# W_o and the third part of x and C, each by seven products, in a float32 encoder block on one core

## The chip, the cores and the metric

The kernel runs on one core of a Trainium2 chip. Its time is the device time of one execution in microseconds (us). Before the change the median of three runs is 1026.59 us (1026.17 to 1027.6). The core has five engines with queues of their own, each served in order: TensorE (PE in the profile, with its weight loads as PEld), VectorE (DVE), ScalarE (ACT), GpSimd (POOL) and SyncE (SP). SP only issues DMAs here. POOL issues DMAs too, among them those that add what they carry to what lies at the destination.

## What is computed

One layer of an encoder on x of 512 tokens by 1024 features, all float32. The parts that the change touches, from the reference:

```python
h = rmsnorm(x, g_mix); proj = h @ w_in
xc, gb, gc, q, k, v, g_sw, gate_a, gate_r = split(proj)
u = gc * xc
conv = sum(u_pad[:, tap:tap + s] * w_conv[tap] for tap in range(3))
y_a = (gb * conv) @ w_a_out
ret = retention forward + backward over 4 heads of q, k, v
y_r = (groupnorm(ret) * silu(g_sw)) @ w_r_out
m = sigmoid(gate_a) * y_a + sigmoid(gate_r) * y_r
x = x + m @ w_o
h2 = rmsnorm(x, g_ffn)
x = x + (silu(h2 @ w_ff_gate) * (h2 @ w_ff_up)) @ w_ff_down
return rmsnorm(x, g_final)
```

## The kernel before

**Products.** Every float32 operand is kept as a high and a low part, hi + lo, and a product takes three matmuls: hi·hi, hi·lo, lo·hi. `split` makes the two parts: ScalarE casts to hi (L200), VectorE subtracts to get lo (L201). Matmuls write PSUM banks of 128 x 512, of which there are eight.

**Seven products.** Much of the work is done on 2 x 2 quarters by Strassen's scheme in Winograd's form: seven products of quarters in place of eight, at the price of sums of quarters of both operands (named s1 to s4 for the activations, t1 to t4 for the weights) and of the results. `strassen` (L434) does it token-major with 512 columns (the value and gate quads, W_a, `down`): 24 matmuls of 512 columns per product. `fm_quad` (L383) does it feature-major through `prod` (L372): 24 matmuls of 256 columns per product. W_o (L1037 to L1058) and the third and fourth part of the convolution (`do_mix`, L801) are plain: W_o has 192 matmuls of 512 columns, and x, C and B of one part 48 each.

**Weights.** `plan` lists all units of weights in the order of use. A "q" entry is one quarter or sum of quarters, a "c" entry a plain block of two units. SP loads them into ten `raw` tiles of 128 x 1024 (512 KB; L283 for quarters, L240 for blocks), some `LEAD` = 4 entries ahead. For a sum like t1 = b11 + b12 VectorE adds two raw tiles (L298). Then `split` fills one of five `whi` and `wlo` buffers. A raw tile comes free when its remainder is made, a whi/wlo pair when its last matmul is done.

**Sums made in DRAM.** For the quads named in `SUMMED` (the first two of the feed-forward, `("f", 0)` and `("f", 1)`) the sums t1 to t4 are made ahead by DMAs on POOL's queue: eight steps a quad, a copy (L271) and then an adding copy (L269) for each of four sums. Each step is queued behind a store of a value or gate quad (`sum_step`, called at L745 and L754): three per quad, six quads.

**Order.** Value and gate quads (to about 324 us), the convolution's first two parts (`mix_quads`: x and C of part 0, of part 1, B of both), loads of head 0 and its scores, part 2 (`do_mix(2)`), then per head the product with v, group norm (POOL takes the power -1/2, L890) and the product with W_r, W_a by `strassen`, merge, W_o, feed-forward, final norm. The order of instructions on each engine is set by a list scheduler when the program is built, from the order in which the code makes them and the readiness it models; `tc.issue_after` adds an edge on one engine.

**W_o before.** `turn(0)` and `turn(1)` transpose the merged m on TensorE (L981) and split it out of PSUM. Four banks collect each half of W_o. For each block of 128 tokens `ev_o` adds the residual (L1003), stores the row block, takes squares on ScalarE, a power on POOL, and scales (L1015); `tr_o` transposes the normed block (L1030) and makes its parts (L1033 to L1035) for the feed-forward, whose first products are `first_tokens`. One block of W_o lies in a `big` tile in place of whi/wlo buffers. There are fourteen `big` tiles, and nine `t` tiles of 128 x 512.

## Time and profile before

| | |
|---|---|
| Median of 3 runs | 1026.59 us |
| The profiled execution | 1027.93 us, its span 1026.1 us |
| TensorE busy | 1018.1 us, 99% of the span, 5610 matmuls |
| VectorE busy | 886.3 us, 86% |
| ScalarE busy | 535.5 us, 52% |
| GpSimd busy | 125.0 us, 12% |
| Granted TensorE clock | 0.999 |

The profile is one execution. A page gives busy time by engine, the chain that ended last, and groups of instructions; the trace behind it can be asked for waits, for stretches of time and for single instructions. A name such as "L201 DVE TENSOR_TENSOR wlo<-raw,whi" is line 201 on VectorE, writing `wlo` from `raw` and `whi`. A busy matmul includes its pipeline, so successive matmuls overlap in the rows, and their rate is read from the chain.

### The profile page before, as it was taken

To read this page: it belongs to the slowest core of one execution; us is meant where nothing else is said; L and a number is where in the kernel's file an instruction comes from. 1 tells how busy PE (TensorE), PEld (TensorE's weight loads), DVE (VectorE), ACT (ScalarE), POOL (GpSimd) and SP (SyncE) were. 2 spreads that over 40 slices of the span, in tenths; PEclk is the share of its full clock that TensorE was granted. 3 is DMA by queue.
4 is the path that set the end of the run, shared out by engine and by line. 5 is a ranking of instruction groups with operands and counts; after the bars stand their busy time and mean duration, and the time that the engine had idled before them with its cause. 6 is when DMAs were issued, how large, how long until landed. Compare 5 with 4: busy or idle time off the path is not lost.

```text
span 1026.1 us, 14780 instructions
## 1 busy us (share of the span) xinstructions
PE 1018.1 (99%) x5610; PEld 887.9 (87%) x5610; DVE 886.3 (86%) x1151; ACT 535.5 (52%) x728; POOL 125.0 (12%) x205
## 2 busy tenths in 40 slices
PE   9999999999999999999999999999999999999997
PEld 7888888888888998888888888889998999899986
DVE  7878998969798988797999998569998999889996
ACT  7547655553656455342542334356654565556554
POOL 0030231222212003202011000000002000110011
PEclk9999999999999999999999999999999999999999
DMA  9525597794767657828177525633318522663513
GB/s 346 195 83 183 172 299 211 213 312 153 255 203 238 254 200 256 323 81 314 52 277 285 208 94 176 236 102 121 122 44 220 177 87 83 193 156 103 164 29 96
DMA packets 51304, 187.66 MB, mean 183 GB/s; under 512 B 6880, under 2 KB 7008, under 8 KB 47264
## 3 DMA queue, kind: packets, MB, share of 16 engines
q1 hardware_dynamic: 36448, 133.19, 37.5%
q0 software_dynamic: 14496, 53.23, 17.5%
q8 instruction: 44, 0.72, 0.3%
q10 hardware_dynamic: 288, 0.29, 0.1%
q14 instruction: 28, 0.23, 0.1%
HBM read 148.14 MB, written 46.92 MB: 190 GB/s over the span
## 4 chain that ended last, share of the span: by engine, by line
PE 97%; DVE 1%; DMA 1%; issue 0%; POOL 0%; ACT 0%; POOLq 0%; DVEq 0%; ACTq 0%
PE bank L424 34%; PE bank L380 28%; PE bank L339 11%; PE bank L341 11%; PE bank L340 11%; DMA raw<-wquad 1%; PE bank L470 0%; PE bank L1030 0%; PE bank L981 0%; PE bank L655 0%; DVE wlo L201 0%; DVE raw L298 0%; DVE big L1229 0%; DVE t L445 0%; POOL fin L1219 0%
## 5 line engine op out<-in xcount | busy, mean ns | idle before, releaser
L200 ACT CAST whi<-raw 128x1024 fp32r<-128x1024 f32 (+2 forms) x291 | 294.5, 1028 | 278.7 <-PE bank L424 60.0
L201 DVE TENSOR_TENSOR wlo<-raw,whi 128x1024 fp32r<-128x1024 f32 (+2 forms) x292 | 343.9, 1193 | 81.6 <-ACT whi L200 81.1
L380 PE MATMUL bank<-xform,whi 128*128 128x256 f32 x1424 | 257.6, 284 | 0.2 <-ACT whi L200 0.2
L380 PEld LDWEIGHTS bank<-xform,whi 128*128 128x128 f32 x1424 | 222.4, 192 | 1.2 <-ACT t L431 0.5
L380 PE MATMUL bank<-xform,wlo 128*128 128x256 f32 x712 | 201.5, 283 | 0.0
L424 PE MATMUL bank<-whi,big 128*128 128x512 f32 x596 | 187.6, 390 | 0.0
L298 DVE TENSOR_TENSOR raw<-raw 128x1024 f32<-128x1024 f32 (+1 forms) x128 | 152.1, 1206 | 3.8 <-DMA raw<-wquad 2.8
L380 PEld LDWEIGHTS bank<-xform,wlo 128*128 128x128 f32 x712 | 136.8, 192 | 0.0
L424 PEld LDWEIGHTS bank<-whi,big 128*128 128x128 f32 x596 | 112.0, 188 | 23.8 <-ACT t L431 0.4
L424 PE MATMUL bank<-whi,xform 128*128 128x512 f32 x384 | 121.3, 390 | 0.0
L424 PE MATMUL bank<-wlo,big 128*128 128x512 f32 x298 | 116.2, 390 | 0.0
L431 ACT COPY t<-bank 128x512 f32<-128x512 f32 x105 | 61.0, 585 | 56.3 <-PE bank L380 29.7
L339 PE MATMUL bank<-big,whi 128*128 128x512 f32 x220 | 85.8, 390 | 0.0
L341 PE MATMUL bank<-big,wlo 128*128 128x512 f32 x220 | 85.7, 390 | 0.0
L340 PE MATMUL bank<-big,whi 128*128 128x512 f32 x220 | 85.7, 390 | 0.0
L424 PEld LDWEIGHTS bank<-whi,xform 128*128 128x128 f32 x384 | 72.1, 188 | 15.1 <-DVE xform L201 0.2
L424 PE MATMUL bank<-wlo,xform 128*128 128x512 f32 x192 | 74.8, 390 | 0.0
L339 PE MATMUL bank<-whi,big 128*128 128x512 f32 x176 | 69.0, 392 | 0.0
L340 PE MATMUL bank<-wlo,big 128*128 128x512 f32 x176 | 68.6, 390 | 0.0
L341 PE MATMUL bank<-whi,big 128*128 128x512 f32 x176 | 68.2, 390 | 0.0
L424 PEld LDWEIGHTS bank<-wlo,big 128*128 128x128 f32 x298 | 56.0, 188 | 11.4
L340 PEld LDWEIGHTS bank<-big,whi 128*128 128x128 f32 x220 | 41.3, 188 | 8.6
(205 smaller groups left out, 1394.8 us busy)
## 6 DMA issues: line engine op xcount, KB each, us to landing
raw<-wquad SPq DMA_DIRECT2D x132, 512.0 KB, 4.6
raw<-wpack SPq DMA_DIRECT2D x50, 512.0 KB, 5.3
z<-t POOLq DMA_DIRECT2D x24, 256.0 KB, 4.7
zform<-z POOLq DMA_DIRECT2D x6, 1024.0 KB, 6.0
v<-t POOLq DMA_DIRECT2D x16, 256.0 KB, 5.3
sg<-t POOLq DMA_DIRECT2D x16, 256.0 KB, 5.0
qh<-t POOLq DMA_DIRECT2D x16, 256.0 KB, 3.0
ql<-t POOLq DMA_DIRECT2D x16, 256.0 KB, 3.6
```

The costliest lines, as they stand in the source:

```text
L200: first = (round or nc.scalar.copy)(hi, src)
L201: nc.vector.tensor_tensor(out=lo, in0=src, in1=hi.bitcast(F32), op=ALU.subtract)
L298: nc.vector.tensor_tensor(out=t, in0=t, in1=raws[quad, more, u][:, 0:n], op=ALU.add)
L339: nc.tensor.matmul(ps, lh, rh, start=first, stop=False)
L340: nc.tensor.matmul(ps, lh, rl, start=False, stop=False)
L341: nc.tensor.matmul(ps, ll, rh, start=False, stop=last)
L380: nc.tensor.matmul(o, l[:, c], r[:, k], start=start and s == 0 and k == 0 and i == 0, stop=stop and k == 3 and i == 2, skip_group_check=True)
L424: nc.tensor.matmul(pss[tt], l, r[:, c], start=start and k == 0 and i == 0, stop=stop and k == n - 1 and i == 2, skip_group_check=True)
L431: nc.scalar.copy(t, ps)
```

## The change

Both plain products become seven. For x and C of part 2, `xc_quad(2)` runs as a third `fm_quad` behind B of the first parts; `do_mix(2)` is left with B of part 2. For W_o, `behind` hooks into `strassen` of W_a: behind its s3 product m's a11 is transposed, behind its a22 product m's a22, then W_o's first product runs, then m's a21 is transposed and s1 and s2 are formed, ahead of W_a's last product. The other five products of W_o follow, with the transposes of a12 inside the second. `turn` now makes one quarter, and `form`, which was the feed-forward's, makes a sum of quarters and its parts. Each product's result goes to the residual by `join` at once, and `complete` does what `ev_o` did when a row block's half is whole.

Both weights join `SUMMED`. The sums of x and C go first among those behind the value and gate quads, and a step now stands behind every second store (four per quad). W_o's sixteen steps stand behind the sixteen powers of the heads. Head 0 is loaded behind `xc_quad(2)`, and weight blocks after that are queued behind its second load (`behind` in `prefetch_block`). All W_o units use the whi/wlo buffers.

```diff
-    for c0, c1 in ((C_XC, C_GC), (C_XC + 256, C_GC + 256), (C_GB, C_GB + 256)):
+    for c0, c1 in ((C_XC, C_GC), (C_XC + 256, C_GC + 256), (C_GB, C_GB + 256), XC[1:]):
         for name in FORMS:
             out.append(("q", ("x", c0, c1), name, 0, 4))
     for s in (2, 3):
-        for c in (C_XC, C_GC, C_GB):
+        for c in (C_GB,) if s == 2 else (C_XC, C_GC, C_GB):
             a("w_in", c + s * 256)
     for h in range(HEADS):
         for c in (0, 512):
             b("w_r_out", h * VD, 4, c, 512)
-    for name in FORMS:
+    for kind, name in [("a", x) for x in FORMS[:6]] + [("o", "b11"), ("a", "b22")] + [
+            ("o", x) for x in ("t1", "t2", "b21", "b22", "t3", "t4")]:
         for u in (0, 2):
-            out.append(("q", ("a",), name, u, 2))
-    for r in (0, 512):
-        for c in (0, 512):
-            b("w_o", r, 4, c, 512)
+            out.append(("q", (kind,), name, u, 2))
...
-SUMMED = (("f", 0), ("f", 1))
+SUMMED = (XC, ("f", 0), ("f", 1), ("o",))
...
+            with tc.issue_after(behind[-1].ins) if behind else nullcontext():
+                nc.sync.dma_start(st[c], wpack[i][:, c * QH:(c + 1) * QH])
...
+    def sums_of(quads):
+        return [(quad, f, g, u, add) for group in (
+            (("t1", "b11", 0), ("t3", "b22", 0)), (("t1", "b12", 1), ("t3", "b12", 1)),
+            (("t2", "t1", 0),), (("t2", "b22", 1),), (("t4", "t2", 0),), (("t4", "b21", 1),))
+            for quad in quads for f, g, add in group for u in parts(quad)]
+
+    steps = {"quads": sums_of(SUMMED[:1]) + sums_of(SUMMED[1:3]), "heads": sums_of(SUMMED[3:])}
+
+    def sum_step(behind, among="quads"):
+
+        if steps[among]:
...
+        if behind:
+            behind(5)
         prod_tm(n, forms["a22"], a, False, True)
         for tt in range(2):
             ev21(tt, a[tt])
...
-                if tt and not o:
+                if tt:
...
+    def xc_quad(s, c):
+
+        u, got = u_tile(), {}
+
+        def ev21(ps):
+            nc.vector.tensor_tensor(out=u[:, :, 257:513], in0=halves(ps), in1=halves(got["c2"]), op=ALU.mult)
+
+        def ev12(t):
+            nc.vector.tensor_tensor(out=u[:, :, 1:257], in0=halves(got["x1"]), in1=halves(t), op=ALU.mult)
+        fm_quad(xf, lambda t: got.update(x1=t), ev21, lambda t: got.update(c2=t), ev12)
+        for m in range(2):
+            conv(m, 2 * s + m, u[:, m], c[:, m])
...
+        part2.append(bigtile()[:, 0:2, :])
+        xc_quad(2, part2[0])
+        head = load_head(0)
+
+        behind.append(last[1])
+        return head
+
+    def do_mix(s):
+        if s == 2:
+            c = part2[0]
...
+            power = nc.gpsimd.tensor_tensor(out=mv[:, 3:4], in0=mv[:, 2:3], in1=mhalf[:, 0:1], op=ALU.pow)
+            sum_step(power, "heads")
...
+        name = f"a{th + 1}{half + 1}"
+        if not m32:
+            t = [bigtile(), bigtile()]
+            for j in range(4):
+                m32[f"a{j // 2 + 1}{j % 2 + 1}"] = t[j // 2][:, j % 2 * 2:j % 2 * 2 + 2, :].rearrange(
+                    "p a (b c) -> p (a b) c", c=256)
+        if name != "a21":
+            M[name] = form_tile()
+        for tt in range(2):
             ps = bank()
             for k in range(4):
-                nc.tensor.transpose(ps[:, k * P:(k + 1) * P], sga[half][:, nb, k * P:(k + 1) * P], ident)
+                nc.tensor.transpose(ps[:, k * P:(k + 1) * P], sga[half][:, 2 * th + tt, k * P:(k + 1) * P], ident)
             ps = ps.rearrange("p (k t) -> p k t", k=4)
-            sl = slice(nb * P, (nb + 1) * P)
-            split(ps, hi[:, :, sl], lo[:, :, sl])
-    strassen(4, zf, merge(0, 0), merge(0, 2), merge(1, 2), merge(1, 0))
-    turn(0)
-
+            sl = slice(tt * P, (tt + 1) * P)
+            if name != "a21":
+                split(ps, *(t[:, :, sl] for t in M[name]))
+            nc.scalar.copy(m32[name][:, :, sl], ps)
+
+    def form(out, name, o, in0, in1, op):
+        nc.vector.tensor_tensor(out=o, in0=in0, in1=in1, op=op)
+        out[name] = form_tile()
+        split(o, *out[name])
...
+    def join(nb, half, ps, op=ALU.add):
+
+        yt = y[half][:, nb, :]
+        nc.vector.tensor_tensor(out=yt, in0=yt, in1=ps, op=op)
+
+    def complete(nb, half, last):
+        yt, ac = y[half][:, nb, :], acs[nb]
+        nc.sync.dma_start(ydr[nb * P:(nb + 1) * P, half * 512:(half + 1) * 512], yt)
+        nc.scalar.activation(t512(), yt, AF.Square, accum_out=ac[:, last:last + 1])
+        if not last:
+            nc.vector.tensor_scalar(out=ac[:, 3:4], in0=ac[:, 0:1], scalar1=1.0 / D, scalar2=EPS,
+                                    op0=ALU.mult, op1=ALU.add)
...
+        hs[nb] = [t512(), t512()]
+        for j, h in enumerate(hs[nb]):
+            nc.vector.scalar_tensor_tensor(out=h, in0=y[j][:, nb, :], scalar=ac[:, 5:6],
+                                           in1=gb[:, j * 512:(j + 1) * 512], op0=ALU.mult, op1=ALU.mult)
...
+    po = {}
+
+    def behind(i):
+        if i == 5:
+            turn(0, 0)
+            return
+        turn(1, 1)
+        po["a"] = [bank(), bank()]
+        prod_tm(4, of(M["a11"]), po["a"], True, False, lambda tt: join(tt, 0, po["a"][tt]))
+        turn(0, 1)
+        form(M, "s1", m32["a22"], m32["a21"], m32["a22"], ALU.subtract)
+        form(M, "s2", m32["a22"], m32["a22"], m32["a11"], ALU.subtract)
+    strassen(4, zf, merge(0, 0), merge(0, 2), merge(1, 2), merge(1, 0), behind)
+    a, d, b = po["a"], [bank(), bank()], [bank(), bank()]
+    prod_tm(4, of(M["s1"]), d, True, False, lambda tt: join(2 + tt, 1, d[tt]))
+
+    def ev(tt):
+        join(tt, 1, a[tt], ALU.subtract)
+        if tt == 0:
+            turn(1, 0)
+    prod_tm(4, of(M["s2"]), a, False, False, ev)
+    form(M, "s4", m32["a12"], m32["a12"], m32["a22"], ALU.add)
+
+    def ev(tt):
+        join(tt, 0, b[tt])
+        complete(tt, 0, 0)
+    prod_tm(4, of(M["a12"]), b, True, True, ev)
+    form(M, "s3", m32["a21"], m32["a11"], m32["a21"], ALU.subtract)
+
+    def ev(tt):
+        join(tt, 1, d[tt])
+        complete(tt, 1, 1)
+    prod_tm(4, of(M["s4"]), d, False, True, ev)
+
+    def ev(tt):
+        join(2 + tt, 1, a[tt], ALU.subtract)
+        complete(2 + tt, 1, 0)
+        if tt == 0:
+            tr_o(0)
+    prod_tm(4, of(M["s3"]), a, False, False, ev)
+
+    def ev(tt):
+        join(2 + tt, 0, a[tt])
+        complete(2 + tt, 0, 1)
+        if tt == 0:
+            tr_o(1)
+    prod_tm(4, of(M["a22"]), a, False, True, ev)
...
     first_tokens(*FIRST_PRODUCTS[0])
+    tr_o(2)
     first_tokens(*FIRST_PRODUCTS[1])
-    tr_o(NB - 1, hs[NB - 1])
...
+    tr_o(3)
```

More of the change, by code (lines that the diff above doesn't have):

```diff
@@ L1 @@
-from contextlib import ExitStack
+from contextlib import ExitStack, nullcontext
 import numpy as np
@@ L147, with parts @@
 BLOCKS, FIRST = BLOCKS[1:], BLOCKS[0]
-SUMMED = (("f", 0), ("f", 1))
+SUMMED = (XC, ("f", 0), ("f", 1), ("o",))
+def parts(quad):
+    return (0, 2) if quad == ("o",) else (0,)
 def loads():
@@ L163, in loads @@
                 out.append((i, quad, need, u, nk * WIDTH[quad[0]]))
-    return out + [(len(PLAN), quad, "b12", 0, 4 * WIDTH[quad[0]]) for quad in SUMMED]
+    return out + [(len(PLAN), quad, "b12", u, QH) for quad in SUMMED for u in parts(quad)]
 LOADS = loads()
@@ L311, in prefetch @@
         if x[0] == "c":
-            units = prefetch_block(loads, splits, x[1] == "w_o" and x[2] == 512 and x[4] == 512)
+            units = prefetch_block(loads, splits)
         else:
@@ L454, in strassen @@
             ev21(tt, a[tt])
+        if behind:
+            behind(6)
         prod_tm(n, forms["s4"], d, False, True)
@@ L1291, in pack_weights, with pack_quads @@
     return out
-def pack_quads(w_in, w_a, gate, up, down):
+def pack_quads(w_in, w_a, w_o, gate, up, down):
     out = np.zeros((len(QUARTERS), P, QH), np.float32)
```

148 lines of the change are left out of this document (46 added, 102 removed).

## The prediction, made before the changed kernel was run

> **What bounds the kernel now.** The page comes first: how busy each engine is, and the chain that ended last.
>
> ```profile
> span 1026.1 us, 14780 instructions
> ...
> PE 1018.1 (99%) x5610; PEld 887.9 (87%) x5610; DVE 886.3 (86%) x1151; ACT 535.5 (52%) x728; POOL 125.0 (12%) x205
> ...
> PE 97%; DVE 1%; DMA 1%; issue 0%; POOL 0%; ACT 0%; POOLq 0%; DVEq 0%; ACTq 0%
> ```
>
> TensorE (PE) is busy 1018.1 of 1026.1 us and 97% of the chain. Next the waits of TensorE alone (engine, line, whom it waited for, us in total, times, longest):
>
> ```profile
> PE bank L470 <- DVE t L467: 1.4, 1, 1.4
> PE bank L380 <- ACT whi L200: 0.2, 1, 0.2
> ```
>
> Only 1.6 us of waiting in the whole span, 1.4 of it the very first. A matmul less therefore is time less, and nothing else in the change can win more than the other 0.2 us. Then the chain in order of time (start, us, what):
>
> ```profile
> 323.62 55.15 PE bank L380 x456
> ...
> 602.38 38.08 PE bank L424 x168
> 640.46 1.75 PE bank L981 x16
> ...
> 775.09 0.50 issue
> ...
> 791.42 74.16 PE bank L380 x614
> ```
>
> A 512-wide matmul takes 38.08/168 = 0.2267 us, a 256-wide one in the projections 55.15/456 = 0.1209, eight transposes 1.75/2 = 0.875. The break from 775.09 to 791.42 is a loop through a late weight load which TensorE's own work just covers. Last the stages around the two edits (from:to, length; busy us and instructions of PE, its weight loads, DVE, ACT, POOL; granted clock, DMA share, GB/s):
>
> ```profile
> 323.60:378.60 55.00, 55.00 (x457) 54.67 (x456) 49.04 (x58) 28.22 (x36) 2.68 (x5) 1.00 0.60 216
> 378.60:422.90 44.30, 44.30 (x219) 37.44 (x218) 33.96 (x52) 19.27 (x28) 10.53 (x16) 1.00 0.84 304
> 623.70:640.50 16.80, 16.80 (x76) 13.87 (x76) 16.80 (x24) 7.38 (x9) 0.00 (x0) 1.00 0.51 168
> 640.50:677.60 37.10, 37.10 (x180) 30.35 (x179) 20.23 (x28) 13.03 (x21) 0.56 (x1) 1.00 0.59 201
> 677.60:690.70 13.10, 13.10 (x73) 11.17 (x71) 9.68 (x18) 9.21 (x21) 1.08 (x2) 1.00 0.24 91
> 690.70:720.00 29.30, 29.30 (x246) 29.19 (x245) 27.11 (x31) 19.77 (x28) 0.54 (x1) 1.00 0.44 135
> 720.00:763.00 43.00, 43.00 (x352) 42.59 (x351) 40.99 (x56) 26.50 (x38) 0.00 (x0) 1.00 0.26 84
> ```
>
> 623.7 is the end of W_a's fourth product (a12), 690.7 the first feed-forward product. VectorE (DVE) is the second engine: full in 623.7 to 640.5, with much air from 640.5 to 690.7 and hardly any from there to 763. That air is what the change spends.
>
> **TensorE's saving.** W_o was 2 halves x 8 k x 4 row blocks x 3 = 192 matmuls, and becomes 7 x 24 = 168: 24 x 0.2267 = 5.44 us. The third part of x and C was 2 x 48 = 96 matmuls of 512 columns and becomes 7 x 24 = 168 of 256: 96 x 0.2267 - 168 x 0.1209 = 21.76 - 20.31 = 1.45 us. The 32 transposes of `turn` stay 32. Together 6.9 us. The Trainium skill (TensorE: Matmul & The Clock Gate, Back-to-back issue gap) gives an isolated warm matmul columns/2.4 + 2.5 ns, 215.8 and 109.2 ns here; an estimate from that page makes the second part 20.7 - 18.3 = 2.4 us, so the sum 0.9 us better. The rows are 5% and 11% above these figures, and the saving by the rows stands.
>
> **VectorE's bill in the W_o stage.** Prices (start, us, line and form, count):
>
> ```profile
> 655.65 2.48 DVE L201 TENSOR_TENSOR big<-bank,big 128x512 fp32r<-128x512 f32 x4
> ...
> 687.48 1.42 DVE L1015 SCALAR_TENSOR_TENSOR t<-big,ac,gb 128x512 f32<-128x512 f32 x2 [0.65 <-POOL ac L1011]
> ...
> 712.09 3.49 DVE L201 TENSOR_TENSOR wlo<-raw,whi 128x1024 fp32r<-128x1024 f32 x3
> ```
>
> That is 0.62 us for a 128x512 operation out of PSUM, 0.71 for a scaling and 1.16 for a 128x1024 operation. Added: 14 weight units instead of 8, already summed in DRAM, 6 x 1.16 = 7.0; 14 `join`s instead of 8 evictions, 6 x 0.62 = 3.7; four sums of m with their remainders, 8 x 1.16 = 9.3. Removed: the remainders of the a21 block, 2 x 0.62 = 1.2. Net +18.8 us. From 623.7 to 690.7 VectorE now works 16.80 + 20.23 + 9.68 = 46.7 of 67.0 us. Behind the first feed-forward product go token block 2's scaling (1.4, the second row) and, on TensorE, its eight transposes (0.87): 46.7 + 18.8 - 1.4 = 64.1 us of work, against 67.0 - 5.44 - 0.87 = 60.7 us of TensorE. VectorE is 3.4 us short there. The next two stages have 29.3 + 0.9 - 27.1 - 1.4 = 1.7 and 43.0 - 41.0 = 2.0 us of air: paid back at 763, with 0.3 over.
>
> Whether that stalls TensorE depends on the lead of the weights. ScalarE (ACT), 602.4 to 720, by form:
>
> ```profile
> L200 ACT CAST whi<-raw 128x1024 fp32r<-128x1024 f32 x30 | 31.4, 1051 | 47.2 <-PE bank L341 17.2 <-PE bank L424 15.7 <-PE bank L380 8.4
> L431 ACT COPY t<-bank 128x512 f32<-128x512 f32 x11 | 6.4, 585 | 3.2 <-PE bank L424 3.2
> ...
> L200 ACT CAST xform<-big 128x1024 fp32r<-128x1024 f32 x4 | 4.1, 1048 | 0.0
> ```
>
> The casts of weights wait for TensorE to give a buffer back: the five buffers are full. With two in use, three are ready, 3 x 2.72 = 8.2 us of lead (a unit is half of a 5.44 us product), more than 3.4. What the lead does not cover is work that TensorE wants at once. s1 of m has one product (5.44 us) between the last transpose of a21 and its use, and takes a last copy 0.59, an add 1.2, a cast 1.05 and a remainder 1.2: 4.0 us, some 4.4 with hops, so 1 us of margin on a queue that is full and whose pieces last 1.2. The transposes of a12 have 5.44 + 2.72 = 8.2 us behind W_a's last product; in that time VectorE must do its six merge operations (3.7), s2 (2.4), two weights (2.3), one `join` (0.6): 9.0. The token blocks' scalings wait for POOL's power as now. No row shows these waits. Lower bound: 0, where the order of the queue puts them ahead of the weights. Upper bound: s1 late by two 1.2 us pieces beyond its margin (1.4), a12 late by 0.8 and a piece (2.0), the two later sums and the scaling a piece each (3.6): 7.0. I take 2.0, nearer to 0, because from 623.7 to 640.5 a queue as full as that, with the same evictions and weights, cost TensorE nothing. ScalarE gets 6 casts, 8 copies and 4 large casts less 2 small ones, some 14 us, onto 13.0 + 9.2 of 50.2 us: room enough.
>
> **The x,C quad.** Seven finished weight units instead of four (3 x 1.16) and three more combinations (3 x 0.62): +5.4 us on 49.0 + 34.0 of 99.3 us, less 1.45 of time: 90%, no loss taken; without that air at most 5.4. Head 0's five loads move on SP's queue behind the quad's seven. The last of them is issued early now:
>
> ```profile
> 351.94 0.37 SPq L848 DMA_DIRECT2D big<-sg  x1
> ```
>
> Scores start at 378.6 now, and then only behind a further 20.3 us of products; four `big` tiles stay free for these loads (eight of xg and xf, two of the convolution, of fourteen). Nothing is taken; if they came only behind the quad, the slowest landing below, 9.3, would show. The weight blocks that now follow the second load on SP are needed later still. SP also issues nine weight loads more (six for W_o, three here) at some 0.4 us; the stores of y stay eight.
>
> **The sum steps.** 24 more on POOL, eight in the value and gate quads, sixteen behind the heads' powers. An issue, the landings (last column, us), and head 2's first and third power:
>
> ```profile
> 221.74 0.84 POOL L269 DMA_DIRECT2D t2f<-wquad  x1
> ```
>
> ```profile
> t2f<-t1f POOLq DMA_DIRECT2D x2, 512.0 KB, 5.9
> t2f<-wquad POOLq DMA_DIRECT2D x2, 512.0 KB, 9.3
> ```
>
> ```profile
> 516.74 0.54 POOL L890 TENSOR_TENSOR bnmv<-bnmv,mhalf 128x1 f32<-128x1 f32 x1 [29.51 <-DVE bnmv L889]
> ...
> 520.22 0.54 POOL L890 TENSOR_TENSOR bnmv<-bnmv,mhalf 128x1 f32<-128x1 f32 x1 [1.20 <-DVE bnmv L889]
> ```
>
> An adding issue is 0.84 us. With one quad's steps in a row, one to a product, each waits for the one before: an add 5.9 - 5.4 = 0.5, the next copy 9.3 - 5.4 = 3.9, the last add 0.5 again. Behind it on POOL stand the next stores, which free `t` tiles; nine of these against two per product leave it covered, 0; uncovered 3.9. In heads 2 and 3 the third step comes 3.5 us after the copy it adds to, and a landing needs 5.9: POOL stands 2.4 us, and the fourth power, ScalarE's scaling and the transposes behind it are as late. A product of W_r (96 matmuls, 21.8 us) lies between these and their use, so 0; W_o's last sum is loaded some 80 us later. By the Trainium skill (DMA: Bandwidth & Descriptors, Anatomy of one DMA) such a transfer takes 2.0 us + bytes/436e3, 3.2 us here, and POOL would not stand; the rows are twice that, and decide.
>
> **Sum.** The profiled execution took 1027.93 (span 1026.1 and 1.83 around it): 1027.93 - 6.9 + 2.0 = 1023.0. It stood 1.34 above the median of 1026.59, so 1021.7 for the runs.
>
> **Rivals.** (1) Nothing is given back: 1026.59 - 6.9 = 1019.7. For it, the lead of 8.2 us; against it, s1's margin of 1 us. (2) The slower side, VectorE becomes the bound of the W_o stage. It has 64.1 us of work; if it keeps busy less than the whole time, the lead is used up at a share of 64.1/(60.7 + 8.2) = 93%, and the whole saving at 64.1/(68.9 + 6.9) = 85%: the kernel is slower from there. In 677.6 to 690.7, where it waits on ScalarE and POOL in turn, it was 9.68/13.10 = 74% busy; halfway, at 79.5%, the work takes 80.6 us and 11.7 are lost: 1026.59 - 6.9 + 11.7 = 1031.4. Against it: 100% in 623.7 to 640.5. The granted clock is 1.00 in all these stages; by the Trainium skill (TensorE: Matmul & The Clock Gate, What's actually happening) an idle window of some 3.4 us halves it, which no row here shows, and a window at half speed would by an estimate cost a further 1.7 us. (3) VectorE's 3.4 us are not paid back by 763 and arrive at the loop of 775 to 791, which has no slack: half the lead carried there, 4.1, gives 1025.8. Against it, the 3.7 us of air before. (4) POOL's stand of 3.9 us in the quads reaches TensorE: 1025.6. (5) The saving is not there, because the products are more or wider than I count: 1026.6. The counts speak against it.
>
> **How the numbers follow.** Forecast 0.43 (1020.7 to 1024.4, from 1.0 to 4.7 given back), (1) 0.17, (2) 0.21, (3) 0.13, (4) 0.04, (5) 0.02. A measurement here tells 0.2%, 2.05 us. Faster than 1024.5: 0.43 + 0.17 = 0.60. Same: (3) to (5) and little of (2), 0.20. Slower than 1028.6: the rest of (2), 0.20. The range goes from 0.9 under (1), the spread of the runs, to 1030.0, so that half of (2) and a little of (1) are left out, 0.15.
>
> **What would show it.** TensorE 5658 matmuls (5610 - 24 + 72), more than that and (5) holds. TensorE's waits 3 to 4 us in total, at the first product on m's s1 and the transposes of a12; if they stand instead on weights from `whi` and VectorE is under 85% busy in the stage, (2). From the end of W_a's a12 product to the first feed-forward product 62.7 us; 60.7 is (1). A wait of TensorE near the third part of the first `down` is (3). POOL waits before its second-quad sum copies with a wait of TensorE or ScalarE on `t` behind them: (4). I am wrong in kind if the x,C quad or head 0's scores make TensorE wait.

## The result, and the profile after

The changed kernel takes **1037.05 us** (median of 5 runs, 1036.71 to 1039.18) against 1026.72 us of the kernel before in the same session (5 runs, 1026.17 to 1027.8): a ratio of **1.0103, 95% interval 1.0091 to 1.0115**. It is slower by 10.3 us. 1021.7 was forecast, and the result lies above the range.

The page of the changed kernel (span; busy time by engine):

```profile
span 1035.5 us, 14976 instructions
...
PE 1014.3 (98%) x5658; PEld 886.1 (86%) x5658; DVE 906.9 (88%) x1175; ACT 551.1 (53%) x748; POOL 143.9 (14%) x229
...
PE 40%; DVE 5%; issue 2%; ACT 1%; POOL 1%; DMA 0%; POOLq 0%; DVEq 0%
```

The last row is the chain's share by engine; the page follows this chain back only to about 520 us, so its shares do not add up to 100%. TensorE issues 5658 matmuls and is busy less than before, although the span grew by 9.4 us. So the work shrank as planned, and time is lost in waits. Those of TensorE in the changed kernel (engine, line, whom it waited for, us in total, times, longest):

```profile
PE bank L389 <- ACT t L440: 9.5, 3, 7.3
PE bank L483 <- DVE t L480: 1.4, 1, 1.4
PE bank L348 <- DVE big L958: 1.4, 1, 1.4
PE bank L348 <- ACT big L956: 0.7, 1, 0.7
PE bank L389 <- DVE xform L207: 0.6, 1, 0.6
PE bank L389 <- DVE wlo L207: 0.4, 1, 0.4
PE bank L1073 <- DVE t L1060: 0.3, 1, 0.3
PE bank L389 <- ACT xform L1076: 0.2, 1, 0.2
```

L389 is the matmul of `prod`, L440 the copy of `snap`, L348 the plain product, L956 and L958 the evictions of `do_wr`, L207 the subtraction of `split`, L1073 the transposes of `tr_o`. Before there were 1.6 us of waits, 1.4 of them the very first of the span, which is L483 here. The 9.5 us are new, and lie in one place. Two rows of the groups by form, the first and last start in each, mark the stages: the convolution's first product, and W_a's. Before:

```profile
L380 PE MATMUL bank<-big,whi x16: 277/283/284, 323.5 to 326.1; 128*128 128x256 f32 x16
...
L424 PE MATMUL bank<-whi,zform x112: 388/390/393, 602.2 to 640.1; 128*128 128x512 f32 x112
```

And after:

```profile
L389 PE MATMUL bank<-big,whi x16: 278/283/283, 322.7 to 325.4; 128*128 128x256 f32 x16
...
L433 PE MATMUL bank<-whi,zform x112: 389/389/476, 615.3 to 661.3; 128*128 128x512 f32 x112
```

From the convolution to W_a it was 602.2 - 323.5 = 278.7 us and is 615.3 - 322.7 = 292.6 us; 278.7 - 1.45 = 277.3 was due, so **15.3 us are lost there**. From W_a to the end it was 1026.1 - 602.2 = 423.9 and is 1035.5 - 615.3 = 420.2: 3.7 us won where 5.44 were saved.

The stretches of the changed kernel around the wait (columns as in the prediction):

```profile
378.00:392.00 14.00, 14.00 (x117) 13.85 (x116) 13.69 (x21) 7.99 (x11) 5.64 (x9) 1.00 1.00 399
392.60:399.90 7.30, 0.07 (x1) 0.00 (x0) 4.74 (x9) 3.23 (x5) 3.72 (x6) 0.80 0.94 364
400.00:403.00 3.00, 3.00 (x14) 3.00 (x15) 0.67 (x1) 0.00 (x0) 0.68 (x2) 0.50 0.65 217
403.00:405.00 2.00, 1.80 (x12) 1.59 (x11) 0.00 (x0) 0.28 (x1) 0.00 (x0) 0.80 0.02 4
```

TensorE stands for 7.3 us, in the third product of the x,C quad, and then works at a granted clock of 0.50. ScalarE in that time (start, us, line, form; idle before and what ended it):

```profile
392.63 1.04 ACT L206 CAST whi<-raw 128x1024 fp32r<-128x1024 f32 x1 [1.36 <-issue]
395.20 0.62 ACT L206 CAST t<-t 128x512 fp32r<-128x512 f32 x1 [1.52 <-DMA z<-t]
396.80 0.62 ACT L206 CAST t<-t 128x512 fp32r<-128x512 f32 x1 [0.98 <-DMA z<-t]
398.07 0.41 ACT L206 CAST t<-big 128x256 fp32r<-128x256 f32 x1 [0.66 <-DMA z<-t]
399.36 0.59 ACT L440 COPY t<-bank 128x512 f32<-128x512 f32 x1 [0.88 <-DMA z<-t]
```

The last row is the quad's first `snap`, whose bank TensorE waits for. It stands behind the last casts of the z forms of parts 0 and 1 (L206, `t<-t` and `t<-big`). Each of these waits for a `t` tile, and a `t` tile comes free only when a store of z has landed ("<-DMA z<-t"). The same casts of the kernel before:

```profile
392.49 0.62 ACT L200 CAST t<-t 128x512 fp32r<-128x512 f32 x1 [3.28 <-DVE t L796]
395.15 0.62 ACT L200 CAST t<-t 128x512 fp32r<-128x512 f32 x1 [2.04 <-DVE t L201]
395.68 0.40 ACT L200 CAST t<-big 128x256 fp32r<-128x256 f32 x1
```

They dragged on there too, to 396.1, and it was landings that VectorE's part of the same work stood for:

```profile
394.39 0.69 DVE L201 TENSOR_TENSOR t<-t,t 128x512 fp32r<-128x512 f32 x1 [1.18 <-DMA z<-t]
396.00 0.69 DVE L201 TENSOR_TENSOR t<-t,t 128x512 fp32r<-128x512 f32 x1 [0.92 <-DMA z<-t]
```

But TensorE was at head 0's scores then, which need nothing of ScalarE, and waited for nothing. The change put in that place a quad whose third product needs a copy from ScalarE. The landings are also longer than before. The DMA rows (KB each, median us to landing over all four parts), before and then after:

```profile
z<-t POOLq DMA_DIRECT2D x24, 256.0 KB, 4.7
```

```profile
z<-t POOLq DMA_DIRECT2D x24, 256.0 KB, 7.2
```

For the stores of parts 0 and 1 alone (those issued from 376 to 402) the medians are 4.7 and 6.5 us. Head 0's loads now leave SP together, four transfers of 1 MB of which this is the last (before, it left at 351.94):

```profile
377.14 0.61 SPq L879 DMA_DIRECT2D big<-sg  x1
```

The DMA engines are full from 378 to 392 (share 1.00 in the first stretch above), when the z stores are to land; before, the share was 0.86 to 0.99 there. Whether these loads are what lengthens the landings is asked below.

### The profile page after: what moved, and what is told of

Read it like the earlier page. It is cut to its first block, busy times and chain, and to the rows that moved or that the text cites. A ratio compares the mean times of both kernels' runs of the same rounds, so it can differ in the third digit from the quotient of the medians.

```text
span 1035.5 us, 14976 instructions
## 1 busy us (share of the span) xinstructions
PE 1014.3 (98%) x5658; PEld 886.1 (86%) x5658; DVE 906.9 (88%) x1175; ACT 551.1 (53%) x748; POOL 143.9 (14%) x229
## 5 line engine op out<-in xcount | busy, mean ns | idle before, releaser
L206 ACT CAST whi<-raw 128x1024 fp32r<-128x1024 f32 (+2 forms) x302 | 305.6, 1028 | 244.8 <-PE bank L433 63.1
L207 DVE TENSOR_TENSOR wlo<-raw,whi 128x1024 fp32r<-128x1024 f32 (+2 forms) x303 | 355.6, 1190 | 61.6 <-ACT whi L206 60.1
L389 PE MATMUL bank<-xform,whi 128*128 128x256 f32 x1488 | 271.1, 285 | 9.7 <-ACT t L440 8.8
L389 PEld LDWEIGHTS bank<-xform,whi 128*128 128x128 f32 x1488 | 233.4, 193 | 11.3 <-ACT t L440 9.8
L389 PE MATMUL bank<-xform,wlo 128*128 128x256 f32 x744 | 210.8, 284 | 0.4 <-DVE wlo L207 0.4
L433 PE MATMUL bank<-whi,big 128*128 128x512 f32 x596 | 187.5, 390 | 0.0
L433 PE MATMUL bank<-whi,xform 128*128 128x512 f32 x496 | 157.2, 391 | 0.0
L389 PEld LDWEIGHTS bank<-xform,wlo 128*128 128x128 f32 x744 | 143.3, 193 | 0.6 <-DVE wlo L207 0.6
L433 PE MATMUL bank<-wlo,big 128*128 128x512 f32 x298 | 116.0, 389 | 0.0
L433 PEld LDWEIGHTS bank<-whi,xform 128*128 128x128 f32 x496 | 93.0, 188 | 19.8 <-DVE xform L207 0.6
L433 PE MATMUL bank<-wlo,xform 128*128 128x512 f32 x248 | 96.5, 389 | 0.0
L440 ACT COPY t<-bank 128x512 f32<-128x512 f32 x106 | 61.7, 587 | 58.3 <-PE bank L389 32.9
L348 PE MATMUL bank<-big,whi 128*128 128x512 f32 x188 | 73.3, 390 | 0.0
L350 PE MATMUL bank<-big,wlo 128*128 128x512 f32 x188 | 73.2, 389 | 0.0
L349 PE MATMUL bank<-big,whi 128*128 128x512 f32 x188 | 73.1, 389 | 0.0
L433 PEld LDWEIGHTS bank<-wlo,xform 128*128 128x128 f32 x248 | 46.6, 188 | 9.6
L348 PE MATMUL bank<-whi,big 128*128 128x512 f32 x128 | 49.9, 390 | 1.4 <-DVE big L958 1.4
L350 PE MATMUL bank<-whi,big 128*128 128x512 f32 x128 | 49.9, 390 | 0.1
L349 PE MATMUL bank<-wlo,big 128*128 128x512 f32 x128 | 49.8, 389 | 0.0
```

The lines of the kernel that those rows point to most:

```text
L206: first = (round or nc.scalar.copy)(hi, src)
L207: nc.vector.tensor_tensor(out=lo, in0=src, in1=hi.bitcast(F32), op=ALU.subtract)
L348: nc.tensor.matmul(ps, lh, rh, start=first, stop=False)
L349: nc.tensor.matmul(ps, lh, rl, start=False, stop=False)
L350: nc.tensor.matmul(ps, ll, rh, start=False, stop=last)
L389: nc.tensor.matmul(o, l[:, c], r[:, k], start=start and s == 0 and k == 0 and i == 0, stop=stop and k == 3 and i == 2, skip_group_check=True)
```

## The experiments

The theory: the loss is the quad's `snap` behind casts that wait for z stores. Its rivals are VectorE as the bound of the W_o stage (the prediction's slower side), W_o's sum steps on GpSimd in the heads, and head 0's late burst of loads by itself. Line numbers shift by a few between the kernels; the names of the tiles stay. The kernel before ran beside each set, at 1026.74 to 1027.5 us, and ratios are to it. The stretches are read in each kernel's profiled execution as above: from the convolution's first product to W_a's, and from there to the end of the span. The diffs are excerpts against the changed kernel, the last one against W_o alone; "..." stands for what is left out.

| kernel | time, us | ratio (95%) | to W_a | W_a to end |
|---|---|---|---|---|
| before | 1026.72 | | 278.7 | 423.9 |
| the change | 1037.05 | 1.0103 (1.0091 to 1.0115) | 292.6 | 420.2 |
| W_o alone | 1024.56 | 0.9977 (0.9967 to 0.9986) | 279.7 | 420.2 |
| x,C quad alone | 1040.31 | 1.0134 (1.0119 to 1.0149) | 290.4 | 424.0 |
| head 0 loaded earlier | 1031.62 | 1.0051 (1.0034 to 1.0068) | 285.4 | 420.3 |
| W_o's sums in the quads | 1048.04 | 1.0211 (1.0194 to 1.0228) | 290.1 | 420.6 |
| z forms behind the quad | 1027.06 | 0.9997 (0.9988 to 1.0006) | 282.1 | 420.4 |
| both repairs | 1025.76 | 0.9987 (0.9977 to 0.9996) | 281.3 | 420.3 |
| both, z forms later still | 1029.71 | 1.0026 (1.0015 to 1.0036) | 286.8 | 420.2 |
| ten `t` tiles | 1034.33 | 1.0069 (1.0052 to 1.0086) | 289.0 | 420.3 |
| W_o alone, no sum steps | 1023.07 | 0.9966 (0.9954 to 0.9979) | 278.7 | 419.9 |
| both repairs, no low half of z | 1022.85 | 0.9962 (0.9948 to 0.9976) | 277.3 | 420.3 |
| both repairs, low half on POOL | 1033.65 | 1.0064 (1.0051 to 1.0076) | 287.8 | 420.2 |
| W_o alone, sums reordered | 1023.52 | 0.9964 (0.995 to 0.9977) | 278.7 | 420.0 |

### W_o alone

```diff
-    for c0, c1 in ((C_XC, C_GC), (C_XC + 256, C_GC + 256), (C_GB, C_GB + 256), XC[1:]):
+    for c0, c1 in ((C_XC, C_GC), (C_XC + 256, C_GC + 256), (C_GB, C_GB + 256)):
...
-SUMMED = (XC, ("f", 0), ("f", 1), ("o",))
+SUMMED = (("f", 0), ("f", 1), ("o",))
...
-        part2.append(bigtile()[:, 0:2, :])
-        xc_quad(2, part2[0])
...
```

> W_o by seven products alone, its sums behind the heads' powers as in the change; x and C of part 2 plain, as before. Theory A (the loss sits in the x,C quad, the W_o stage gives back about 2 us as forecast, and POOL's standing behind the heads' sum steps costs about 4 us): 1026.7 - 5.4 + 1.7 + 4 = 1027, and no wait of TensorE at a snap of the x,C quad. Rival B (VectorE is the bound of the W_o stage): 1030 or more. Rival C (the heads lose their 4 us to the late loads of the x,C quad and not to the sum steps): 1023.

x, C and B of part 2, and head 0's loads, are as before. Measured: 1024.56 us, faster than before, and the last stretch is the 420.2 us of the whole change. VectorE as the bound of W_o is refuted. The heads cost 1.0 us more than before and not the 4 us of theory A, whose 1027 is missed by 2.4; this is taken up below.

### The x,C quad alone

```diff
-SUMMED = (XC, ("f", 0), ("f", 1), ("o",))
+SUMMED = (XC, ("f", 0), ("f", 1))
...
-    M, m32 = {}, {}
...
-    def turn(half, th):
...
+    def turn(half):
...
```

> The x,C quad of part 2 alone, with its sums first behind the quads and head 0's loads behind it; W_o plain, as before. Theory A: 1026.7 - 1.45 + 11.4 (9.5 of waits, some 1.9 of halved clock) = 1036.7. Rival B: about 1025, the loss being in the W_o stage. Rival C: 1036.7 + 4 = 1040.7.

W_o, its transposes and its part of the plan are those of the kernel before. Measured: 1040.31 us, so the quad alone makes the loss and more. The time is nearer to the second figure, but not for its reason. By the trace 9.1 us are again waits for `snap` (L445 here), and beside the very first wait of the span only 0.2 us of others is left:

```profile
PE bank L394 <- ACT t L445: 9.1, 3, 6.9
```

So the heads lost next to nothing, and the second figure's 4 us are not there. Of the 3.6 us above theory A's 1036.7 the trace shows a part: the granted clock was 0.50 from 394.8 to 405.05, so that some 5.2 us of work ran at half speed, an estimated 2.6 us where 1.9 were expected. The rest is open; the profiled execution, 1039.15, was the fastest of four.

### Head 0 loaded earlier

```diff
+        head = load_head(0)
         fm_quad(xf, times(0, T1), times(0, T2), times(1, T2), times(1, T1))
...
         xc_quad(2, part2[0])
-        head = load_head(0)
```

> The whole change, but head 0 is loaded ahead of the quad of B instead of behind the x,C quad. Theory A1 (the quad's first snap waits for a t tile because the z stores land late, and they land late because head 0's 4.4 MB share the DMA engines with them): the waits of 9.5 us at the snaps go, the z stores land in some 5 us again instead of 7, and the time is 1037 - 11.4 = 1025.7. Rival A2 (nine t tiles are too few whatever the loads do, because z_forms stands ahead of the snap on ScalarE): the wait stays, 1035 to 1037.

Measured: 1031.62 us, between the two. The wait for `snap` falls from 9.5 to 4.3 us and does not go. The first row is TensorE's wait, the second the copy that it waits for, the third the landings:

```profile
PE bank L389 <- ACT t L440: 4.3, 1, 4.3
```

```profile
402.10 0.58 ACT L440 COPY t<-bank 128x512 f32<-128x512 f32 x1 [2.49 <-DMA z<-t]
```

```profile
z<-t POOLq DMA_DIRECT2D x24, 256.0 KB, 7.3
```

The landings did not get shorter, against theory A1: 7.3 us in the median, and 6.6 for the stores of parts 0 and 1, with head 0's loads long done. Ten weight loads of 512 KB are under way between 376 and 402 here, where the changed kernel has head 0's four loads and two of these. Nor did the copy come sooner: it starts 8.6 us after the end of the quad's second product (393.5), in the changed kernel 6.7 us (399.36 after 392.7). What changed is what TensorE did meanwhile. From 393.5 to 398.3 it worked on head 0's scores, whose operands were there: 4.8 us of work inside the gap, and 5.4 us came back in all. So the early loads fill a part of the gap; they do not close it.

### W_o's sums behind the quads' stores

```diff
-                if tt:
-                    sum_step(last)
+                sum_step(last, "quads" if tt else "heads")
...
-            sum_step(power, "heads")
```

> The whole change, but W_o's sixteen sum steps stand behind the first stores of the value and gate quads instead of behind the heads' powers. Theory A (the heads' stage loses about 4 us because POOL stands at a sum step that waits for the one before, with the power behind it): 1037 - 4 = 1033, and TensorE's waits at L348 in the heads go. Rival C (the heads lose it to the loads that pile up behind the x,C quad): 1037. Rival D (the DMA engines are full in the quads already, and eight more MB there make the raw loads late): over 1037.

Measured: 1048.04 us. TensorE now waits in the value and gate quads:

```profile
PE bank L433 <- DVE wlo L207: 3.2, 2, 2.4
PE bank L433 <- ACT whi L206: 2.6, 1, 2.6
PE bank L433 <- ACT t L440: 2.3, 1, 2.3
```

The convolution begins 11.6 us later than in the changed kernel (334.36 against 322.72). The DMA share from 130 to 324 us is 0.86 where it was 0.80, and the transfers from the weights into `t_o`, copies and adding ones together, land in 9.3 us where they took 8.6. In that stage 16 more transfers of 512 KB cost 11.6 us. In the heads the waits of `do_wr` fall from 2.1 to 0.3 us and the stretch to W_a by 2.5, so the theory is right about that place.

### The z forms behind the quad

```diff
-        for s in range(2):
-            z_forms(s, c[:, s])
         part2.append(bigtile()[:, 0:2, :])
         xc_quad(2, part2[0])
+        for s in range(2):
+            z_forms(s, c[:, s])
         head = load_head(0)
```

> The whole change, but the z forms of the convolution's parts 0 and 1 (their casts on ScalarE, subtractions on VectorE, and 16 stores of z) are emitted behind the x,C quad instead of ahead of it; head 0's loads stay behind the quad. Theory A (the quad's snap of p1 stands on ScalarE behind casts of the z forms, which wait for `t` tiles that only landing z stores free): the wait of 9.5 us on ACT's snap is gone, and with it the stretch at half clock, so 10 us or more come back: 1025 to 1028 us. Theory B (head 0's burst of 4.4 MB is what fills the DMA engines, whoever stands in line): the weight tiles or head 0's scores now wait for that burst; of the 15.3 us lost at most 5 come back: 1032 us or more.

Measured: 1027.06 us: 10 us come back by moving instructions alone, with the same loads at the same time.

```profile
PE bank L348 <- ACT big L956: 1.4, 1, 1.4
PE bank L348 <- DVE big L958: 1.3, 1, 1.3
PE bank L389 <- ACT t L440: 0.7, 1, 0.7
```

Of 9.5 us of the wait for `snap` 0.7 is left. The place of the z forms ahead of the quad's copies is the cause; the burst, with no z form in line ahead, costs 1.3 us at most (the run with both repairs below is faster by that).

### Ten `t` tiles

```diff
-    tmp = ctx.enter_context(tc.tile_pool(name="tmp", bufs=9))
+    tmp = ctx.enter_context(tc.tile_pool(name="tmp", bufs=10))
...
-    ones = const.tile([P, P], F32, name="ones")
+    ones = t512()[:, 0:P]
...
-    lw = const.tile([P, 6, 8], F32, name="lw")
+    lw = t512()[:, 0:48].rearrange("p (a b) -> p a b", b=8)
```

> The whole change with ten `t` tiles instead of nine (the room comes from two small constants, moved into tiles that stood free). Theory A (a shortage of `t` tiles holds the casts ahead of the snap): the tenth tile lets one more cast of eight go ahead of a landing, so that the wait of 9.5 us falls by 0.7 to 4 us (one store's pace on POOL, or up to half a landing of 7.2 us): 1033 to 1036.5 us. Theory B (the burst alone): no change within 0.7 us, 1036.4 to 1037.8 us.

Measured: 1034.33 us, 2.7 us less than the change, inside the bounds of the shortage of tiles and outside those of the burst alone:

```profile
PE bank L389 <- ACT t L440: 8.7, 3, 6.6
```

The wait for `snap` shortens by 0.8 us in all, the lower end of what the theory allowed. The rest of the gain is elsewhere: the 2.1 us of waits in `do_wr` are gone, which no side expected. So the time inside the theory's bounds is in part luck. A shortage of `t` tiles shows, and one more is not enough.

### Both repairs

```diff
+        head = load_head(0)
         fm_quad(xf, times(0, T1), times(0, T2), times(1, T2), times(1, T1))
-        for s in range(2):
-            z_forms(s, c[:, s])
         part2.append(bigtile()[:, 0:2, :])
         xc_quad(2, part2[0])
-        head = load_head(0)
+        for s in range(2):
+            z_forms(s, c[:, s])
```

> The whole change with both repairs: head 0 loaded ahead of the quad of B, and the z forms of parts 0 and 1 behind the x,C quad. If order on ScalarE and the loads are the whole loss of the stage (15.3 us), the stage comes back to the 278.75 us of before less 1.45, and the time to that of W_o alone less 1.4: 1023 us. If the x,C quad costs something of its own (5.4 us more work of VectorE, as the prediction bounded it), 1025 to 1029 us.

Measured: 1025.76 us. The wait for `snap` is gone. What stays is a cost of the quad's own: 281.3 us to W_a, 4.0 over the 277.3 due, of which 1.0 is also in W_o alone. The waits that are left in this stretch have VectorE behind them (and 0.3 us ScalarE):

```profile
PE bank L349 <- DVE big L207: 1.3, 1, 1.3
PE bank L348 <- DVE big L958: 1.2, 1, 1.2
```

### The z forms later still

```diff
+        early.append(c)
...
     vv, sg = split_v(nxt[2]), nxt[3]
+    for s in range(2):
+        z_forms(s, early[0][:, s])
     do_mix(2)
```

> As the run with both repairs, but the z forms of parts 0 and 1 come still later, behind head 0's scores and the split of its v. If with both repairs head 0's scores wait behind the z forms on ScalarE and VectorE, this takes that wait away and is 1 to 4 us faster than it; if the z forms are covered there, the two are within 1 us.

Measured: 1029.71 us, 4 us slower than with both repairs, which neither side expected. TensorE waits 4.3 us, at 459 us, for a weight's remainder in the convolution's fourth part:

```profile
L350 PE MATMUL bank<-big,wlo 128*128 128x512 f32 x188 | 74.5, 396 | 4.3 <-DVE wlo L207 4.3
```

On VectorE this remainder (462.5) stands directly behind the sixteen transposes of head 0 (L221, 449.2 to 462.3); with both repairs these began at 446.0 and nothing waited. TensorE then ran at a granted clock of 0.50 from 463.1 to 469.9. That the later z forms push the transposes back is likely, but no run shows it by itself.

### Both repairs, without the low halves of z

```diff
-            hl = [t512(F32R)[:, 0:256 * n].rearrange("p (f t) -> p f t", f=n) for _ in range(2)]
-            split(t, *hl)
+            hl = [t512(F32R)[:, 0:256 * n].rearrange("p (f t) -> p f t", f=n)] * 2
+            nc.scalar.copy(hl[0], t)
...
```

> The version with both repairs (head 0 loaded ahead of the quad of B, z forms of parts 0 and 1 behind the x,C quad), with the low halves of z left out: the 16 subtractions on VectorE that make them are gone, and the high half is stored in their place (as many stores and bytes). So VectorE has some 10 us less to do between the quad and the last head. If what the x,C quad still loses (3.0 us: 281.3 us from the convolution's first product to W_a's, where 279.7 less 1.45 was due) is VectorE running late behind the quad's own 5.4 us, the waits for VectorE of 1.3 and 1.2 us shrink by half or more, and the time falls by 1.5 to 3 us: 1023 to 1024.3 us. If it is something else (POOL's powers, loads), 1025 to 1026 us.

Measured: 1022.85 us, and the stretch to W_a is 277.3 us, the due value:

```profile
L389 PE MATMUL bank<-big,whi x16: 278/283/283, 323.5 to 326.1; 128*128 128x256 f32 x16
...
L433 PE MATMUL bank<-whi,zform x112: 389/389/476, 600.8 to 646.8; 128*128 128x512 f32 x112
```

Of the waits that the run with both repairs had in this stretch none remains, and the sum steps, which this kernel still has, cost nothing either, although GpSimd still stands 6.0 us for landings in `t_o`. So these waits come from the work around z on VectorE and the tiles it holds, and the quad's saving of 1.45 us is there as soon as that work shrinks. The kernel also takes one `t` tile less for each form, so the part of the tiles and that of VectorE's time are not told apart.

### The low halves of z on GpSimd

```diff
-            split(t, *hl)
+            nc.scalar.copy(hl[0], t)
+            nc.gpsimd.tensor_tensor(out=hl[1], in0=t, in1=hl[0].bitcast(F32), op=ALU.subtract)
...
```

> The version with both repairs, with the 16 subtractions that make z's low halves moved from VectorE to GpSimd. If VectorE is what is late and GpSimd's subtractions go beside it unhindered: as with those subtractions left out, 1023 to 1024.3 us, which would beat both kernels. If GpSimd's own line grows too long (it also issues the z stores, the powers and the sum steps, 16 of some 0.6 us) or slows VectorE down: 1026 us or more.

Measured: 1033.65 us. The groups of GpSimd (count, busy, mean ns of one) and a stretch:

```profile
L803 POOL TENSOR_TENSOR t<-t,t 128x512 fp32r<-128x512 f32 x8 | 11.3, 1414 | 2.3 <-ACT t L802 1.9 <-DMA z<-t 0.4
```

```profile
428.00:432.00 4.00, 4.00 (x11) 3.12 (x10) 4.00 (x4) 0.62 (x1) 1.52 (x2) 0.50 0.56 177
```

A subtraction takes 1.41 us on GpSimd where VectorE takes 0.69, in a line that also holds the stores. And VectorE is slowed: its 1159 instructions are busy 909.6 us, where the same 1159 were busy 899.4 without the low halves. This one, which GpSimd's subtraction at 438.3 overlaps, takes twice the 1.22 us of its kind:

```profile
438.05 2.52 DVE L207 TENSOR_TENSOR wlo<-raw,whi 128x1024 fp32r<-128x1024 f32 x1
```

So both conditions of the expectation's second figure came about, and this run does not tell their shares apart. TensorE waits 4.4 us for VectorE's split of an operand of head 0 (`big`, L207), and the clock falls to 0.50 once more.

### W_o alone, without its sum steps

```diff
-            src = wsum[quad, name, u] if name[0] == "t" else quarter(quad, name, u)
+            src = wsum[quad, name, u] if name[0] == "t" and quad[0] != "o" else quarter(
+                quad, "b11" if name[0] == "t" else name, u)
...
-            sum_step(power, "heads")
```

> The W_o change alone, with W_o's 16 sum steps left out: the four products whose weights are sums load the packed quarter b11 in their place (the same number of bytes), so those weights are not the ones wanted. This prices the sum steps behind the heads' powers. If they cost the 1.0 us by which the stretch from the convolution's first product to W_a's first grew (279.75 us against 278.75), that stretch is 278.8 us again and the time 1023.5 us, 1 us under the run of W_o alone. The prediction's zero for the stand on POOL: 279.75 us still and 1024.5 us.

Measured: 1023.07 us, and 278.7 us to W_a as before the change. The sum steps behind the heads' powers therefore cost 1.0 us in the stretch and 1.5 us in the medians. How, the trace of W_o alone shows (GpSimd in head 2; L914 is the power, L278 and L280 the steps):

```profile
523.65 0.85 POOL L278 DMA_DIRECT2D t_o<-wquad  x1 [4.21 <-DMA t_o<-t_o]
524.25 0.83 POOL L914 TENSOR_TENSOR bnmv<-bnmv,mhalf 128x1 f32<-128x1 f32 x1
```

An adding step waits 4.2 us for the copy it adds to (2.2 in head 3), and the head's fourth power comes only behind it.

### W_o alone, sums in another order

```diff
-    steps = {"quads": sums_of(SUMMED[:2]), "heads": sums_of(SUMMED[2:])}
+    steps = {"quads": sums_of(SUMMED[:2]), "heads": [
+        (("o",), f, g, u, add) for f, g, add in (
+            ("t1", "b11", 0), ("t3", "b22", 0), ("t1", "b12", 1), ("t2", "b22", 0),
+            ("t4", "b21", 0), ("t2", "t1", 1), ("t3", "b12", 1), ("t4", "t2", 1)) for u in (0, 2)]}
```

> The W_o change alone, with its 16 sum steps in another order: t2 and t4 start as copies of b22 and b21 and take the finished t1 and t2 afterwards, so that no step follows one that it needs by fewer than four steps. In the run of W_o alone two steps stood on GpSimd for their predecessors' landings, 6.4 us, with the powers of the last heads behind them. If that stand is the price of the sum steps (leaving them out took 1.05 us off the stretch to W_a and 1.5 us off the time), it goes: 1023.0 to 1023.7 us, the wait of GpSimd on t_o is gone and so is TensorE's wait of 0.7 us for VectorE's sum in the heads. If it is the issuing itself or the traffic of the steps, 1024.2 to 1025 us.

Measured: 1023.52 us (1023.13 to 1024.07), as expected: 3.6 us under the kernel before and 13.5 under the changed one, with everything computed. It is the fastest complete kernel of the study; its interval overlaps that of W_o alone. GpSimd's wait on `t_o` is gone from the trace, and so is TensorE's wait of 0.7 us in the heads: of the waits left, 1.4 us is the very first of the span, and 1.5 lie about the feed-forward's start. The stretch to W_a is 278.7 us, as before the change and as without the steps. So the standing was the price of the sum steps, and not their issue or traffic. This order together with both repairs was not run.

## Why the prediction was wrong

**What bounds the kernel, and TensorE's saving: right.** TensorE bound the kernel, the 5658 matmuls hold, and so do the 6.9 us: TensorE's busy time is 1011.1 us in the run without the low halves of z, against 1018.1 before. The 1.45 us of the quad appear in full where nothing stands in the way (277.3 against 278.7). The estimate by the Trainium skill (TensorE: Matmul & The Clock Gate, Back-to-back issue gap) was 2.4 us for it; the trace went by the rows. That page's figure holds for W_o too, which the prediction left out: by an estimate from it W_o saves 5.2 in place of 5.44 us, and the sum would be 0.7 us better and not 0.9.

**VectorE's bill in the W_o stage: right in sum, near in size, not in place.** 2.0 us were to be given back; the stretch from W_a to the end gives back 5.44 - 3.7 = 1.7. From the end of W_a's a12 product (636.8) to the first feed-forward products (698.45 by the chain) lie 61.7 us, 61.3 without one early piece of 0.4, where 62.7 were forecast and 60.7 would have been the first rival; so only 0.6 to 1.0 us is given back in that stretch. W_o alone adds 16.2 us to VectorE's busy time (902.5 against 886.3), where 18.8 were billed; the quad alone adds 4.0, where 5.4 were. VectorE is about as full as the bill says, in stretches of the changed kernel:

```profile
640.00:660.00 20.00, 20.00 (x102) 16.83 (x101) 19.90 (x26) 13.39 (x20) 0.00 (x0) 1.00 0.49 143
660.00:680.00 20.00, 20.00 (x93) 16.38 (x92) 20.00 (x26) 12.30 (x17) 0.00 (x0) 1.00 0.49 160
680.00:700.00 20.00, 19.41 (x101) 16.03 (x100) 18.72 (x30) 15.43 (x29) 2.56 (x3) 1.00 0.77 260
```

Before, it was 20.23 of 37.10 us busy from 640.5 to 677.6. The waits were to come at s1 of m and the transposes of a12; neither waits at all. They come later, at the feed-forward's first transposes and forms (0.3, 0.2, 0.6 and 0.4 in the list of waits, 1.5 us). It looks as if the lead of the weights carried the shortage past W_o, so that the debt showed where the lead ended; no run shows this by itself. With VectorE 94 to 100% busy, the second rival's 79.5% did not happen.

**The x,C quad: the step that failed.** It said "no loss taken; without that air at most 5.4", and of head 0's loads "Nothing is taken; if they came only behind the quad, the slowest landing below, 9.3, would show", and so the quad entered the sum as a gain of 1.45 us and a loss of nothing. 15.3 us were lost, of which 1.0 belongs to the sum steps below. The step counted VectorE's busy time and the `big` tiles, and looked for head 0's loads at head 0. It did not ask what stands ahead of the quad on ScalarE, and what these instructions wait for:

- The z forms of parts 0 and 1 stand ahead of the quad's `snap`, and wait for `t` tiles freed by landings. These waits were in the trace of before (on VectorE, with ScalarE's casts waiting for VectorE), with nothing behind them that TensorE needed. "Nine of these against two per product" was worked out for the value and gate quads and not for the place where the z forms take two `t` tiles a form, besides v and w, and hold them until a store lands.
- Head 0's loads came too late to be of use in the gap: loaded as early as before, they let head 0's scores fill 4.8 us of it. They also filled the DMA engines while the z stores of parts 0 and 1 were to land, and these landed in 6.5 us in place of 4.7. But the landings were as long (6.6) with the loads out of the way, so what lengthened them stays open, and with it how much of the wait the longer landings make.
- The working out: 9.5 us of the wait; 400.0 to about 403.8 at half clock, 1.9 us by an estimate from the granted clock; 2.1 us of waits in `do_wr`. Together 13.5 of 15.3. The list counts only the time after the last matmul's end. Counted from one matmul's start to the next, less its usual pace, the three gaps at `snap` are 10.0 us (the first, 392.39 to 400.00, is 7.5) and those in the heads 2.8, which with the clock makes 14.7; 0.6 us stay open.

The repairs settle that the z forms' place is the cause: with them moved 10.0 us come back, with the loads moved 5.4, with both 11.3. The bound "at most 5.4" for VectorE's extra work holds for what then remains, 3.0 us beyond W_o alone's 1.0.

**The sum steps: half right.** In the quads GpSimd stood 5.0 us before a copy, where 3.9 was forecast, and 3.1 us before two adding steps; nothing that TensorE waited for came of it. In the heads GpSimd was to stand 2.4 us in each of heads 2 and 3, at no cost behind a product of W_r; in W_o alone it stood 4.2 and 2.2 us, and cost 1.0 to 1.5 us. The product of W_r was to cover that. The other order of the steps shows that the standing is the price; how it reaches TensorE, by way of a late addition on VectorE (0.7 us, L951 of W_o alone), is argued from one wait.

**The rivals and the range.** The slower side was looked for in the W_o stage alone and priced at 1031.4. None of the five rivals had the quad, although the prediction's last sentence named it as the way to be wrong in kind. The clock rule of the Trainium skill (TensorE: Matmul & The Clock Gate, What's actually happening) was priced at 1.7 us for one window at half speed. The trace has such a loss, an estimated 1.9 us, in the x,C quad and not in the W_o stage; its half speed lasted 6.8 us, of which TensorE worked 3.8.

## What to carry to other kernels

When work is put into a place where TensorE was busy with something that needs no other engine, read what the other engines stand waiting for at that place before: a wait that costs nothing there becomes the new work's wait. Follow each of its evictions to the instructions ahead of it on the same queue and to what frees their tiles. And when a load is moved to later, ask not only whether its own use still finds it there, but also which work it keeps from filling a gap.

## What the runs showed of the hardware

**The clock.** In the changed kernel TensorE stood from 392.7 to 400.0 us and was granted half the clock from 397.0 to 403.8: the granted clock is 0.99 from 396 to 397, 0.50 from 397 to 403 and 0.60 from 403 to 404. So it fell 4.3 us after the last matmul and rose 3.8 us after work came back. Read in the same way, the runs with a wait of over 4 us differ in both figures:

| kernel | fall after the last matmul, us | rise after work came back, us | at half clock, us |
|---|---|---|---|
| the change | 4.3 | 3.8 | 6.8 |
| head 0 loaded earlier | 4.2 | 3.3 | 3.4 |
| x,C quad alone | 1.9 | 5.2 | 10.2 |
| W_o's sums in the quads | 3.1 | 2.9 | 6.8 |
| ten `t` tiles | 2.3 | 6.0 | 10.2 |
| both, z forms later still | 3.6 | 6.1 | 6.8 |
| both repairs, low half on POOL | 2.3 | 4.7 | 6.8 |

The times at half clock, however, are one, two or three times 3.4 us. The Trainium skill (TensorE: Matmul & The Clock Gate, What's actually happening) gives a free-running window of some 3.4 us for both directions, and these lengths agree with it. The same section has the fall come after at least one idle window; in the x,C quad alone it came 1.9 us after the last matmul, so there the window was not idle throughout, and the measurement decides.

**DMAs.** In the changed kernel the copies from DRAM to DRAM of 512 KB (L280) landed in 6.6 us and the adding ones (L278) in 8.5 us, in the median of all sums. With W_o's sums in the quads, where the share of the DMA engines was 0.86 for 194 us, it was 7.4 and 9.7 us. The z stores of 256 KB of parts 0 and 1 took 4.7 us in the kernel before, 6.5 in the changed one and 6.6 with head 0 loaded earlier; what sets their landing is not shown.

**VectorE beside GpSimd.** With subtractions on GpSimd, VectorE's operations that take two tiles from outside PSUM were held up when they ran beside one (2.52 us for 1.22 at 438.05, 1.42 for 0.68 at 406.62). Those with an operand in PSUM kept their time (0.68 us at 400.48, 0.74 at 436.54).
